# Row-wise maximum of absolute values of an 8192 x 8192 matrix: tile loads issued from two queues in turn

## The chip, the core and the metric

The kernel runs on one core of a Trainium2 chip. The metric is the device time of one execution in microseconds (us): lower is better. Three runs of the kernel before gave 634.45, 634.63 and 634.87 us, so the median is 634.63 us. Beside these timed runs there is one profiled execution, and every duration below comes from that one. Its span, from the first to the last instruction, is 632.9 us.

## What is computed

The reference takes the infinity norm of every row, which is the largest absolute value in the row:

```python
def setup_inputs():
    return {
        "x": np.random.randn(8192, 8192).astype(np.float32),
    }

def reference(x: np.ndarray) -> np.ndarray:
    return np.linalg.norm(x, ord=np.inf, axis=1)
```

The input has 8192 x 8192 x 4 B = 268.4 MB and every byte is read once. The output is 8192 numbers, 32 KB.

## The kernel before

**Tiling.** The 8192 rows are cut into 64 tiles of 128 rows. Row p of a tile lies in partition p of the on-chip memory, so a whole tile is 128 partitions of 8192 numbers (32 KB in each partition, 4 MB in all). This text counts the tiles from 0 to 63. Tiles live in `xt`, from a pool of five buffers (line 39): tile t takes the buffer that tile t - 5 had, and its first load may start only when VectorE has finished reading that older tile.

**Loop.** For each tile the loop at line 48 walks over the chunks of its columns. For each chunk it issues one load (line 55, on the queue of SP, the engine SyncE) and then one VectorE reduction (line 59), which takes the maximum of the absolute values along the row. Tiles 0 to 53 have one chunk of 8192 columns, and their reduction writes directly into column t of the result tile `res`. The last ten tiles follow the list `COOLDOWN` (line 11):

```python
COOLDOWN = (
    [[4096, 4096]] * 7
    + [[4096, 2048, 2048]]
    + [[2048, 2048, 2048, 2048]]
    + [[2048, 2048, 1536, 1280, 1280]]
)
```

Tiles 54 to 60 have two chunks, tile 61 three, tile 62 four and tile 63 five. The reduction of chunk h of such a tile writes column h of a small tile `partial`, which has five columns and only one buffer (line 46). All ten tiles share it. After its last chunk, each of these tiles has one more VectorE reduction (line 68) that takes the maximum over the used columns of `partial` and writes column t of `res`. This text writes "61 h2" for chunk 2 of tile 61, counting chunks from 0.

**Order.** No order is written out by hand. A framework turns the loop into one instruction list for each engine and adds the waits: a reduction waits for its load, a load waits for the reader of the buffer that it overwrites, and a reduction that writes a column of `partial` waits for the line 68 reduction that read that column for the tile before. Loads report to eight completion semaphores in turn, so that load n also waits for load n - 8. The list for VectorE holds 54 whole-tile reductions, then 26 chunk reductions with ten line 68 reductions between them, in the order of the source. The list for SP holds 80 loads, also in the order of the source, and at its end the store of the output.

**End.** After the last tile `res` (128 x 64) is transposed by TensorE (line 78), copied out of its accumulator by VectorE (line 80) and stored by one DMA (line 81). ScalarE (ACT) has no work in this kernel.

Of the kernel before, what the change touches and what calls it, by code (L numbers as in the profile page):

```python
# [1 line left out]

# [5 lines left out]
# [10 lines that stand above are left out]
@with_exitstack  # L19
def kernel(  # L20
    ctx: ExitStack,
    tc: tile.TileContext,
    x: bass.AP,
    out: bass.AP,
):
    nc = tc.nc
    P = 128
    n_rows, n_cols = x.shape
    assert n_rows % P == 0

    T = n_rows // P
    if n_cols == 8192 and T >= len(COOLDOWN):
        chunks = [[n_cols]] * (T - len(COOLDOWN)) + COOLDOWN
    else:
        chunks = [[n_cols]] * T

    x_t = x.rearrange("(t p) m -> t p m", p=P)

    pool = ctx.enter_context(tc.tile_pool(name="sbuf", bufs=5))
    single = ctx.enter_context(tc.tile_pool(name="single", bufs=1))  # L40
    psum_pool = ctx.enter_context(tc.tile_pool(name="psum", bufs=1, space=bass.MemoryType.PSUM))

    res = single.tile([P, T], mybir.dt.float32)
    maxch = max(len(c) for c in chunks)
    if maxch > 1:
        partial = single.tile([P, maxch], mybir.dt.float32)

    for t in range(T):
        ch = chunks[t]
        assert sum(ch) == n_cols  # L50
        xt = pool.tile([P, n_cols], x.dtype)
        off = 0
        for h, w in enumerate(ch):
            dst = res[:, t : t + 1] if len(ch) == 1 else partial[:, h : h + 1]
            nc.sync.dma_start(  # L55
                out=xt[:, off : off + w],
                in_=x_t[t, :, off : off + w],
            )
            nc.vector.tensor_reduce(  # L59
                out=dst,  # L60
                in_=xt[:, off : off + w],
                axis=mybir.AxisListType.X,
                op=mybir.AluOpType.max,
                apply_absolute_value=True,
            )
            off += w
        if len(ch) > 1:
            nc.vector.tensor_reduce(  # L68
                out=res[:, t : t + 1],
                in_=partial[:, : len(ch)],  # L70
                axis=mybir.AxisListType.X,
                op=mybir.AluOpType.max,
            )

    ident = single.tile([P, P], mybir.dt.float32)
    make_identity(nc, ident)
    res_t_psum = psum_pool.tile([T, P], mybir.dt.float32)
    nc.tensor.transpose(res_t_psum, res, ident)  # L78
    res_t = single.tile([T, P], mybir.dt.float32)
    nc.vector.tensor_copy(out=res_t, in_=res_t_psum)  # L80
    nc.sync.dma_start(out=out.rearrange("(t p) -> t p", p=P), in_=res_t)


# [1 line left out]
_INS = ['x']  # L85
_OUTS = [((8192,), 'float32')]


# [23 lines left out]
```

## Time and profile before

| Quantity | Value |
|---|---|
| Median of three runs | 634.63 us (634.45 to 634.87) |
| Span of the profiled execution | 632.9 us |
| Bytes read by the loads | 268.44 MB, mean 424 GB/s over the span |
| VectorE (DVE) busy | 558.9 us, 88% of the span |
| Whole-tile reductions | 54, mean 8686 ns |
| Chunk reductions of 4096 / 2048 / 1536 / 1280 columns | mean 4416 / 2278 / 1742 / 1476 ns |
| Reductions over `partial` (line 68) | 10, mean 156 ns |
| Whole-tile loads, from issue to landing | 54, median 39.8 us |
| Issue of one load on SP | 80, median 328 ns |

The difference between the median and the profiled span is 634.63 - 632.9 = 1.73 us, which lies around the span. A load's time from issue to landing includes the time that it stands behind earlier loads, so 39.8 us is not what the transfer of one tile takes. "Idle before" in a row of the profile is the time that the engine stood still just ahead of those instructions, with what ended it.

### The profile page before, as it was taken

How to read it: one execution, taken by the hardware profiler on the slowest of the kernel's cores; microseconds unless marked ns; L12 is line 12 of the kernel's file. 1: busy time of each engine (PE TensorE's matmuls, PEld its weight loads, DVE VectorE, ACT ScalarE, POOL GpSimd, SP SyncE). 2: the span in 40 equal slices, each digit the busy share in tenths (PEclk: the TensorE clock that was granted, in tenths of full speed). 3: DMA queues.
4: the chain of work that ended last, by engine and by line, in shares of the span. 5: the costliest groups of instructions: out<-in, count | busy, mean ns of one | idle time of the engine just before them, and what ended most of it. 6: DMA issues, size and time to landing. Idle time of an engine off the chain costs nothing.

```text
span 632.9 us, 294 instructions
## 1 busy us (share of the span) xinstructions
PE 0.4 (0%) x1; PEld 0.1 (0%) x1; DVE 558.9 (88%) x91; POOL 0.7 (0%) x6
## 2 busy tenths in 40 slices
PE   0000000000000000000000000000000000000000
PEld 0000000000000000000000000000000000000000
DVE  1988988988989889889898898898988989999997
POOL 0000000000000000000000000000000000000000
DMA  8999999999999999999999999999999999999995
GB/s 373 439 437 437 433 431 433 431 431 431 431 431 431 431 431 431 431 431 431 431 431 431 431 431 431 431 431 431 431 437 433 435 435 418 427 428 431 425 421 219
DMA packets 11602, 268.49 MB, mean 424 GB/s; under 512 B 1296, under 2 KB 1360, under 8 KB 1744
## 3 DMA queue, kind: packets, MB, share of 16 engines
q1 hardware_dynamic: 11600, 268.47, 98.9%
q14 instruction: 2, 0.02, 0.0%
HBM read 268.44 MB, written 0.03 MB: 424 GB/s over the span
## 4 chain that ended last, share of the span: by engine, by line
DMA 75%; DVE 24%; SPq 0%; issue 0%; PE 0%; DVEq 0%
DMA xt<-in_x_dram 75%; DVE res L59 15%; DVE partial L59 8%; SPq L55 0%; DVE res L68 0%; PE res_t_psum L78 0%; DVE res_t L80 0%; DVEq L59 0%
## 5 line engine op out<-in xcount | busy, mean ns | idle before, releaser
L59 DVE TENSOR_REDUCE res<-xt 128x1 f32<-128x8192 f32 x54 | 469.0, 8686 | 67.6 <-DMA xt<-in_x_dram 67.6
L59 DVE TENSOR_REDUCE partial<-xt 128x1 f32<-128x4096 f32 (+3 forms) x26 | 88.1, 3430 | 2.7 <-DMA xt<-in_x_dram 2.6
L68 DVE TENSOR_REDUCE res<-partial 128x1 f32<-128x2 f32 (+3 forms) x10 | 1.6, 156 | 0.3
L80 DVE COPY res_t<-res_t_psum 64x128 f32<-64x128 f32 x1 | 0.3, 283 | 0.6 <-PE res_t_psum L78 0.6
L78 PE MATMUL res_t_psum<-ident,res 128*64 128x128 f32 x1 | 0.4, 393 | 629.5 <-DVE res L68 629.5
masks.py:199 POOL TENSOR_SCALAR_AFFINE_SELECT ident<-ident 128x128 f32<-128x128 f32 x1 | 0.3, 292 | 0.1
L78 PEld LDWEIGHTS res_t_psum<-ident,res 128*64 128x64 f32 x1 | 0.1, 128 | 629.4 <-issue 629.4
masks.py:197 POOL MEMSET ident<- 128x128 f32 x1 | 0.2, 204 | 0.3 <-POOLq L96 0.3
L96 POOL MEMSET const-bfloat16-1.0<- 128x1 bf16 x1 | 0.1, 101 | 0.0
L96 POOL MEMSET const-uint8-127<- 128x1 uint8 x1 | 0.1, 101 | 0.0
L96 POOL MEMSET const-float32-0.0<- 128x1 f32 x1 | 0.1, 98 | 0.2 <-issue 0.2
L96 POOL MEMSET const-float32-1.0<- 128x1 f32 x1 | 0.1, 98 | 0.0
## 6 DMA issues: line engine op xcount, KB each, us to landing
xt<-in_x_dram SPq DMA_DIRECT2D x54, 4096.0 KB, 39.8
xt<-in_x_dram SPq DMA_DIRECT2D x15, 2048.0 KB, 38.7
xt<-in_x_dram SPq DMA_DIRECT2D x8, 1024.0 KB, 28.3
xt<-in_x_dram SPq DMA_DIRECT2D x2, 640.0 KB, 17.9
xt<-in_x_dram SPq DMA_DIRECT2D x1, 768.0 KB, 19.3
out_dram<-res_t SPq DMA_DIRECT2D x1, 32.0 KB, 1.8
```

What stands on the lines that cost most here:

```text
L59: nc.vector.tensor_reduce(out=dst, in_=xt[:, off : off + w], axis=mybir.AxisListType.X, op=mybir.AluOpType.max, apply_absolute_value=True,)
L68: nc.vector.tensor_reduce(out=res[:, t : t + 1], in_=partial[:, : len(ch)], axis=mybir.AxisListType.X, op=mybir.AluOpType.max,)
L78: nc.tensor.transpose(res_t_psum, res, ident)
L80: nc.vector.tensor_copy(out=res_t, in_=res_t_psum)
L96: nc = _bacc.Bacc("TRN2", target_bir_lowering=False, num_devices=1)
```

## The change

A counter `n_dma` is added that runs over all 80 loads. Loads with an even number are issued from SP as before, loads with an odd number from the queue of ScalarE (ACT). Nothing else in the source differs: chunk sizes, buffers, reductions and the final store (from SP) stay.

```diff
+    n_dma = 0
     for t in range(T):
...
             dst = res[:, t : t + 1] if len(ch) == 1 else partial[:, h : h + 1]
-            nc.sync.dma_start(
+            queue = (nc.sync, nc.scalar)[n_dma % 2]
+            n_dma += 1
+            queue.dma_start(
                 out=xt[:, off : off + w],
                 in_=x_t[t, :, off : off + w],
             )
```

So tiles 0 to 53 alternate between the queues as wholes. Of tiles 54 to 60 chunk 0 goes to SP and chunk 1 to ACT. Of tile 61 chunks 0 and 2 go to SP and chunk 1 to ACT. Of tile 62 chunks 1 and 3 go to SP, 0 and 2 to ACT. Of tile 63 chunks 1 and 3 go to SP, 0, 2 and 4 to ACT.

## The prediction

> **What bounds the kernel now.** I read the page first, then the windows of the end, then the chain of waits. On the page, part 2 and the two costliest groups carry it:
>
> ```profile
> DVE  1988988988989889889898898898988989999997
> DMA  8999999999999999999999999999999999999995
> GB/s 373 439 437 437 433 431 433 431 431 431 431 431 431 431 431 431 431 431 431 431 431 431 431 431 431 431 431 431 431 437 433 435 435 418 427 428 431 425 421 219
> ...
> L59 DVE TENSOR_REDUCE res<-xt 128x1 f32<-128x8192 f32 x54 | 469.0, 8686 | 67.6 <-DMA xt<-in_x_dram 67.6
> L59 DVE TENSOR_REDUCE partial<-xt 128x1 f32<-128x4096 f32 (+3 forms) x26 | 88.1, 3430 | 2.7 <-DMA xt<-in_x_dram 2.6
> ```
>
> The DMA engines are full from the second slice to the last but one, at a steady 431 GB/s. A tile of 4.194 MB takes 4.194 / 0.431 = 9.7 us to load and 8.69 us to reduce, so VectorE waits about 1 us per tile: 67.6 us in all, 12.9 of them before the first tile. The loads set the pace, and VectorE follows closely. The windows show when the last load ends (time, length, busy us of PE, PE's weight loads, VectorE and GpSimd, clock, DMA share, GB/s):
>
> ```profile
> 602.00:617.00 15.00, 0.00 (x0) 0.00 (x0) 14.85 (x7) 0.00 (x0) 1.00 1.01 421
> ...
> 617.00:620.00 3.00, 0.00 (x0) 0.00 (x0) 2.98 (x2) 0.00 (x0) 1.00 1.03 429
> 620.00:622.00 2.00, 0.00 (x0) 0.00 (x0) 1.95 (x2) 0.00 (x0) 1.00 0.99 408
> ...
> 624.00:625.00 1.00, 0.00 (x0) 0.00 (x0) 1.00 (x2) 0.00 (x0) 1.00 1.02 415
> 625.00:626.00 1.00, 0.00 (x0) 0.00 (x0) 1.00 (x1) 0.00 (x0) 1.00 0.27 108
> 626.00:627.00 1.00, 0.00 (x0) 0.00 (x0) 1.00 (x2) 0.00 (x0) 1.00 0.03 10
> ```
>
> Between 625 and 626 the share falls to 0.27, so I set the end of the loads at 625.4 us. The chain, in order of time, shows VectorE's end (start, length, what):
>
> ```profile
> 545.56 8.76 DVE partial L59 x2
> 554.31 0.02 issue
> 554.34 0.17 DVE res L68
> 554.50 0.02 issue
> 554.53 8.76 DVE partial L59 x2
> ...
> 602.09 8.82 DVE partial L59 x3
> ...
> 611.12 8.88 DVE partial L59 x4
> ...
> 620.21 8.94 DVE partial L59 x5
> 629.14 0.02 issue
> 629.17 0.17 DVE res L68
> 629.34 0.14 issue
> 629.47 0.41 PE res_t_psum L78
> ```
>
> VectorE runs without a gap over tiles 61, 62 and 63 and ends at 629.34, only 4 us after the last load. From there to the end of the span are 3.56 us of transpose, copy and store. One tile of the end costs VectorE, from its start to the next tile's: 554.53 - 545.56 = 8.97 us with two chunks, 611.12 - 602.09 = 9.03 (tile 61), 620.21 - 611.12 = 9.09 (tile 62), and 629.34 - 620.21 = 9.13 (tile 63). So little comes after the last load because VectorE reduces in the order in which loads land.
>
> **What the Trainium skill says.** "DMA: Bandwidth & Descriptors", section "Issuing engines are not separate DMA queues": loads from SP and ACT run on the same 16 DMA engines, and a second issuer saves only issue time. The trace before can't show two queues, but it agrees on the second half: an issue takes 328 ns on SP, and the DMA share is 1.00 in mid-kernel, so no issue time is exposed. The section "Queues, rings and completion order" says that each DMA engine takes turns between the queues it has work for, a packet at a time. Here the packets add up: 80 loads of 128 rows are 10,240, the store has 64 rows, and the packets under 512 B are 1,296 = 81 x 16; the sum is the 11,600 of the page. So a packet in the records is one partition's row of one load or one of 16 small ones per DMA. "HBM Reference", section "Specifications (TRN2)": a core that streams alone measures about 425 GB/s, bound by its 16 DMA engines; the trace has 424 in the mean and 431 in the steady part.
>
> **The change part by part.** *Issue.* Forty of 80 issues of 328 ns move from SP to ACT, which is otherwise empty. They lie beside full DMA engines: gain 0. At the start alone up to 0.4 us might be gained (second issue of the chain); I take 0.
>
> *Rate.* No row shows two queues. From above: the best slice has 439 GB/s instead of 431, which would end 265 MB of loads 265 / 0.431 - 265 / 0.439 = 11 us earlier. From below: the shorter rows of the end ran at 408 to 429, in the windows of 617 to 625 some 418, 3% less; if changing between queues cost as much on every row, 19 us would be lost. Since the DMA engines are busy throughout and rows keep their 32 KB, I take 0.
>
> *Landing in pairs.* Tiles 0 and 1 now share the engines and land together, near 21 us instead of 12 and 21. VectorE's first reduction starts some 9 us later, but it has 17.4 us of work for 19.4 us of loads per pair. After a pair lands three loads are still outstanding in five buffers; the first freed buffer comes after 8.7 us and the second after 17.4, both ahead of the next landing at 19.4. Each queue then still holds a load: no DMA idles. Gain and loss 0.
>
> *VectorE's order at the end.* This is where the change costs, and it isn't in the diff. I compared the built instruction lists of both kernels. Before, VectorE's list is the source's. In the changed one three reductions stand ahead of their place. From tile 58 on, with what is moved marked:
>
> ```
> 58 h0, 58 h1, [61 h2], max 58, [62 h3], 59 h0, 59 h1, [63 h4], max 59,
> 60 h0, 60 h1, max 60, 61 h0, 61 h1, max 61, 62 h0, 62 h1, 62 h2, max 62,
> 63 h0, 63 h1, 63 h2, 63 h3, max 63
> ```
>
> These three are the first users of columns 2, 3 and 4 of partial, so no earlier reader holds them back; the scheduler was free to place them early. Each waits for its own load, and VectorE stands still behind it: 62 h3 is the last chunk of tile 62, 63 h4 the last of the whole input. Queued behind 62 h3 are tiles 59, 60, most of 61, 62 and 63; after them TensorE and the store. The loads aren't held: in the built list those of tile 63 need only 58 h1, which stands ahead of all three. So the loads still end at 625.4, with VectorE idle beside them.
>
> When does 62 h3 land? Both queues have 40 loads of 128 rows. With turns row by row the loads land in pairs, one of each queue: 61 h2 (SP) with 62 h0 (ACT), 62 h1 with 62 h2, 62 h3 with 63 h0, 63 h1 with 63 h2, 63 h3 with 63 h4. After 62 h3 there remain 2048 + 1536 + 1280 + 1280 = 6144 columns, 6144 x 512 B = 3.15 MB, at 418 GB/s 7.5 us: it lands at 617.9. The 61 h2 ahead lands 8192 columns = 10.0 us sooner, at 607.9, is reduced in 2.2 us, and VectorE waits again. 63 h4 costs no wait: VectorE reaches it at 617.9 + 2.2 + 8.8 = 628.9, after 625.4.
>
> From 617.9 VectorE has everything from tile 59 on but 61 h2: 2 x 8.97 + 9.03 + 9.09 + 9.13 - 2.22 (a quarter of 8.88) = 42.97 us. It ends at 617.9 + 43.0 = 660.9 instead of 629.34: 31.5 us later. Span 632.9 + 31.5 = 664.4; with the 1.73 us around the span, 666.1 us. The extra semaphore waits in the lists (17 ns each in the trace before) are below 0.2 us together.
>
> The landing of 62 h3 is bounded from both sides: with loads served in the order of issue all of tile 63 (10.0 us) follows it, which gives 615.4 and 663.6 us; with equal bytes to both queues SP, with 2560 columns more than ACT from tile 61 on, ends last, and 3.1 us alone plus 1.9 us shared follow: 620.4 and 668.6 us. I take the middle, since the packet count supports turns by row.
>
> **The rivals.** *Rate better, still slower*: with 439 GB/s all of the end moves up by 11 us, to 655 us. The early slices of 437 to 439 speak for it; DMA share 1.00 at 431 speaks against. *Rate worse, or a starved queue*: up to 19 us more, 685 us. For it: 418 on short rows. Against: rows stay as long as before and each queue keeps a load. *The order does no harm*: VectorE's moved reductions would have to be absent in the run. Then only the pairs act: 61 h0 and h1 land together some 2.4 us later than 61 h0 did at 602.0 (2048 columns, 2.5 us), and VectorE's unbroken 27.3 us end at up to 631.8: 634.6 to 637.1 us. Against: the list is what the engine executes, and the trace before follows its list. *Not slower*: two queues on each DMA engine would have to raise the load rate so far that the late loads land 31.5 us earlier. The place is the whole steady stretch, the point is 268.4 MB / 593 us = 453 GB/s; below it the kernel stays slower. No slice of the profile exceeds 439.
>
> **How the numbers follow.** Forecast, 660 to 673 us: 0.80. Rate better, 650 to 660: 0.07. Rate worse, 673 to 685: 0.09. Order harmless, 634.6 to 637: 0.02. Rate above 453: 0.02. The likeliest is 666 us. The range holds the landing's bounds (663.6 to 668.6) and about 0.7% of the load time on either side for the rate, 4 to 5 us: 659 to 674. A change under 0.2% can't be told from none here. Faster has the last case, 0.02; same takes half of the harmless order, 0.01; slower 0.97.
>
> **What would show it.** VectorE should stand idle in two long stretches between about 590 and 618, released by loads, with the DMA share still near 1 to about 625; then some 43 us of reductions without a gap and no load beside them after 625. Whole-tile reductions should wait in pairs, near 2 us before every second one. Reductions should keep 8.69 us and the steady rate 431 GB/s. I am wrong if the loads end more than 5 us from 625.4, if 63 h4 rather than 62 h3 is the last long wait, or if VectorE's tail is short.

## The result, and the profile after

The changed kernel takes 667.62 us (four runs, 667.31 to 667.69) beside 634.54 us for the kernel before in the same comparison: a ratio of 1.052, 95% interval 1.0505 to 1.0535. Its profiled execution has a span of 665.9 us. The prediction was 666 us, range 659 to 674.

The page of the changed kernel, the lines that answer to those shown of the kernel before:

```profile
DVE  0688889888888988888898888889888899941797
DMA  9999999999999999999999999999999999999500
GB/s 378 441 441 419 431 441 431 419 441 437 421 433 441 431 419 441 433 423 435 441 427 423 441 433 419 439 441 425 425 441 431 419 428 430 428 426 421 230 0 2
...
L62 DVE TENSOR_REDUCE res<-xt 128x1 f32<-128x8192 f32 x54 | 466.5, 8681 | 78.4 <-DMA xt<-in_x_dram 78.4
L62 DVE TENSOR_REDUCE partial<-xt 128x1 f32<-128x4096 f32 (+3 forms) x26 | 87.9, 3429 | 27.9 <-DMA xt<-in_x_dram 27.6
```

The reductions cost what they did (8681 ns against 8686). The DMA engines are as full as before, but they are done two slices before the end, and VectorE has a hole in the slices 36 and 37, while they are still full, that reaches into slice 38. The idle time ahead of the chunk reductions has grown from 2.7 to 27.9 us. The timeline of the same execution (start, length, engine, line, what, count, and in brackets the idle time ahead of it with what ended it) shows where:

```profile
580.74 8.75 DVE L62 TENSOR_REDUCE partial<-xt 128x1 f32<-128x4096 f32 x2
609.52 2.29 DVE L62 TENSOR_REDUCE partial<-xt 128x1 f32<-128x2048 f32 x1 [20.03 <-DMA xt<-in_x_dram]
611.73 0.14 DVE L71 TENSOR_REDUCE res<-partial 128x1 f32<-128x2 f32 x1
619.46 12.34 DVE L62 TENSOR_REDUCE partial<-xt 128x1 f32<-128x2048 f32 x4 [7.59 <-DMA xt<-in_x_dram]
...
662.17 0.16 DVE L71 TENSOR_REDUCE res<-partial 128x1 f32<-128x5 f32 x1
```

At 580.74 VectorE reduces the two chunks of tile 58. Then it waits 20.03 us for one chunk of 2048 columns, 61 h2, finishes tile 58, and waits 7.59 us more for 62 h3. The group "x4" that starts at 619.46 is 62 h3, 59 h0, 59 h1 and 63 h4. From there it runs without a gap until 662.33. The loads are over long before, as the windows of the changed kernel show (columns as in the prediction):

```profile
624.00:625.00 1.00, 0.00 (x0) 0.00 (x0) 1.00 (x1) 0.00 (x0) 1.00 1.02 415
625.00:626.00 1.00, 0.00 (x0) 0.00 (x0) 1.00 (x2) 0.00 (x0) 1.00 0.24 92
...
630.00:666.00 36.00, 0.39 (x1) 0.13 (x1) 32.33 (x19) 0.00 (x0) 1.00 0.00 1
```

So the loads end when they ended before, and 662.33 - 619.46 = 42.9 us of reductions, most of which used to lie beside the loads, now lie behind the wait.

### The profile page after: what moved, and what is told of

It reads as the page before. It is cut to its first block, busy times and chain, and to the rows that moved or that the text cites. A ratio compares the mean times of both kernels' runs of the same rounds, so it can differ in the third digit from the quotient of the medians.

```text
span 665.9 us, 303 instructions
## 1 busy us (share of the span) xinstructions
PE 0.4 (0%) x1; PEld 0.1 (0%) x1; DVE 556.0 (83%) x91; POOL 0.7 (0%) x6
## 4 chain that ended last, share of the span: by engine, by line
DMA 64%; DVE 35%; issue 1%; another core or an unknown queue 0%; PE 0%; SPq 0%
DMA xt<-in_x_dram 64%; DVE res L62 26%; DVE partial L62 8%; DVE res L71 0%; PE res_t_psum L81 0%; SPq L58 0%; DVE res_t L83 0%
## 5 line engine op out<-in xcount | busy, mean ns | idle before, releaser
L62 DVE TENSOR_REDUCE res<-xt 128x1 f32<-128x8192 f32 x54 | 466.5, 8681 | 78.4 <-DMA xt<-in_x_dram 78.4
L62 DVE TENSOR_REDUCE partial<-xt 128x1 f32<-128x4096 f32 (+3 forms) x26 | 87.9, 3429 | 27.9 <-DMA xt<-in_x_dram 27.6
## 6 DMA issues: line engine op xcount, KB each, us to landing
xt<-in_x_dram ACTq DMA_DIRECT2D x1, 768.0 KB, 19.5
```

Of the source, the lines that this page charges most:

```text
L62: nc.vector.tensor_reduce(out=dst, in_=xt[:, off : off + w], axis=mybir.AxisListType.X, op=mybir.AluOpType.max, apply_absolute_value=True,)
```

## The experiments

All of them leave the chunks, the buffers and what each load brings alone. In all but experiment 2, a change in which columns of `partial` are read decides which reductions the scheduler can place early: a reduction that writes a column must stay behind an earlier reader of that column. `partial` is zeroed at the start, and a maximum of absolute values isn't changed by a zero that is read too.

**1. Two queues, VectorE in the order of the source.**

```diff
         partial = single.tile([P, maxch], mybir.dt.float32)
+        nc.gpsimd.memset(partial, 0.0)
...
-                in_=partial[:, : len(ch)],
+                in_=partial[:, :maxch],
```

> Two queues as in the change, but VectorE's list in the order of the source: every reduction over partial reads all five columns (zeroed at the start), so that no chunk reduction can be placed ahead of the tile before it. Theory (the order of VectorE's list is the whole loss): 634.6 to 637.1 us, no wait at the end over 3 us, loads landing until about 627. Rival (two queues cost by themselves, through pairs of tiles landing late or slower loads): most of the loss stays, 650 to 668 us.

Measured: 640.40 us, ratio 1.0091 (1.0076 to 1.0106). Of the 33.1 us, 27.2 are gone with the order alone, and VectorE waits for no load after 527.8 us. The last wait, and the end of VectorE's reductions:

```profile
527.80 17.28 DVE L63 TENSOR_REDUCE res<-xt 128x1 f32<-128x8192 f32 x2 [2.14 <-DMA xt<-in_x_dram]
...
634.87 0.16 DVE L72 TENSOR_REDUCE res<-partial 128x1 f32<-128x5 f32 x1
```

But 5.7 us remain (640.4 - 634.7), more than the 2.4 that the theory allowed and less than the 15 that the rival asked for, so both missed. Experiments 6 and 7 go after the 5.7 us.

**2. One queue, VectorE in the order of the changed kernel.** The loop is written out from tile 58 on, all loads stay on SP, and an ordering edge without a wait ties each reduction from tile 58 on to the one ahead of it.

```diff
...
+    for t in range(59, 64):
+        load(t)
+    chunk(61, 2)
+    last(58)
+    chunk(62, 3)
+    chunk(59, 0)
+    chunk(59, 1)
+    chunk(63, 4)
+    last(59)
...
```

> One queue (SP) for all loads, but VectorE's list in the order that the changed kernel has (61 h2, 62 h3 and 63 h4 ahead of their places). Theory: 62 h3 lands with only tile 63 behind it, 10.0 us ahead of the last landing at 627.1, so at 617.1; 43.0 us of reductions follow: span 663.7, time 665.4 us, some 2 us below the changed kernel. Rival (the second queue is needed for the loss): 634.6 us.

Measured: 665.16 us, ratio 1.048 (1.0465 to 1.0496), 0.2 us from the theory. Its timeline:

```profile
607.04 2.29 DVE L77 TENSOR_REDUCE partial<-xt 128x1 f32<-128x2048 f32 x1 [25.06 <-DMA xt<-in_x_dram]
609.25 0.15 DVE L88 TENSOR_REDUCE res<-partial 128x1 f32<-128x2 f32 x1
616.98 12.33 DVE L77 TENSOR_REDUCE partial<-xt 128x1 f32<-128x2048 f32 x4 [7.59 <-DMA xt<-in_x_dram]
```

The loss appears without a second queue. 62 h3 lands at 616.98, 2.5 us sooner than with two queues, because in one queue only tile 63 stands behind it.

**3 to 5. One moved reduction at a time, two queues.** Each run lets one of the three reductions go ahead of its place. The columns of `partial` that chunks 2, 3 and 4 use are exchanged so that the free one is the last (for 61 h2 and 62 h3), and the tiles ahead read the others:

```diff
+COL = [0, 1, 2, 4, 3]
...
-            dst = res[:, t : t + 1] if len(ch) == 1 else partial[:, h : h + 1]
+            dst = res[:, t : t + 1] if len(ch) == 1 else partial[:, COL[h] : COL[h] + 1]
...
-                in_=partial[:, : len(ch)],
+                in_=partial[:, : 4 if len(ch) < 4 else 5],
```

This is the one for 62 h3. For 61 h2 the list is `[0, 1, 4, 2, 3]` and the condition `len(ch) < 3`; for 63 h4 there is no list, and the tiles read at least four columns.

Only 61 h2:

> Two queues; of the three reductions only 61 h2 stands ahead of its place (the columns of chunks 2, 3 and 4 are exchanged and the earlier tiles read those of chunks 3 and 4 too). Theory (the end is a landing plus the work still queued behind it, and only the worst counts): landing 609.5 + 45.2 of work + 3.56 + 1.73 = 660.0 us. Rival (each wait adds its own idle time, 20.0 us here): 634.5 + 20.0 = 654.5 us.

Only 63 h4:

> Two queues; only 63 h4, the last chunk of the input, stands ahead of its place, now between the chunks and the maximum of tile 60. Theory: VectorE idles until it lands at 627.1, then has 0.2 + 9.03 + 9.09 + 9.13 = 27.45 us left: 654.6 + 3.56 + 1.73 = 659.8 us, though the changed kernel shows no wait at all for this chunk. Rival (what costs nothing in the changed kernel costs nothing alone): 634.6 to 637 us.

Only 62 h3:

> Two queues; of the three reductions only 62 h3 stands ahead of its place, between the chunks and the maximum of tile 58, as in the changed kernel. Theory (a landing plus all the work still queued behind it): 619.4 + 45.2 + 3.56 + 1.73 = 669.9 us, 2.2 us slower than the changed kernel, because 61 h2 is then no longer reduced inside the wait. Rival (the idle time that this wait had in the changed kernel is its price): 634.6 + 7.6 = 642 us.

Measured: 660.28 us with 61 h2 alone (ratio 1.0404, 1.0387 to 1.0421), 659.89 us with 63 h4 alone (1.0397, 1.0382 to 1.0413), and 670.08 us with 62 h3 alone (1.0557, 1.0542 to 1.0571). All three stand within 0.3 us of the theory. The rivals had been put on a base of 634.5 to 637 us; with the order restored the base is 640.4 (experiment 1). On that base the rival for 61 h2 gives 640.4 + 20.0 = 660.4, so this run doesn't tell the two apart. The other two do: 640.4 and 648.0 would have been the rival's times for 63 h4 and 62 h3, and 659.89 and 670.08 were measured. One timeline line of each kernel, in the same sequence:

```profile
609.44 2.29 DVE L66 TENSOR_REDUCE partial<-xt 128x1 f32<-128x2048 f32 x1 [19.80 <-DMA xt<-in_x_dram]
```

```profile
626.88 1.49 DVE L63 TENSOR_REDUCE partial<-xt 128x1 f32<-128x1280 f32 x1 [19.39 <-DMA xt<-in_x_dram]
```

```profile
619.28 2.29 DVE L66 TENSOR_REDUCE partial<-xt 128x1 f32<-128x2048 f32 x1 [29.67 <-DMA xt<-in_x_dram]
```

Compare the brackets with those of the changed kernel. Ahead of 61 h2 the idle time is the same, 19.80 against 20.03 us. Ahead of 62 h3 it is 29.67 instead of 7.59, and ahead of 63 h4 it is 19.39 where the changed kernel shows none. VectorE's work is the same in all of them, so each kernel takes 640.4 us plus the idle time of its own trace: 640.4 + 29.67 = 670.1, for example. But how long that idle time is depends on which early instruction stands first, and what it shows in company says little of what it costs alone. What holds throughout is the landing of the awaited chunk plus the work queued behind it; where several chunks are awaited, the latest of these ends counts. In the changed kernel that is the one of 62 h3, since 61 h2 and 63 h4, which alone end near 660 us, lie before it. With 62 h3 alone the kernel is even 2.5 us slower than with all three moved, since 61 h2 is then no longer reduced inside the idle time (2.2 us by the theory).

**6. The body on two queues, the end on one.** VectorE's order is that of the source, as in experiment 1.

```diff
-            queue = (nc.sync, nc.scalar)[n_dma % 2]
+            queue = (nc.sync, nc.scalar)[n_dma % 2 if t < 54 else 0]
```

> VectorE's list in the order of the source; tiles 0 to 53 alternate between the two queues, tiles 54 to 63 are all on SP. The question is what the 5.7 us of the run with two queues and the source's order are. Theory (the pairs leave VectorE one whole tile behind at 527.8, 8.6 us, of which the end can work off only the 2.9 us that VectorE idles there in the kernel before): the same 640.4 us. Rival (halves of one tile that land together on two queues at the end): back to 634.7 us.

Measured: 640.30 us, ratio 1.0087 (1.0074 to 1.0101). The halves of a tile that land together at the end aren't the cause, since here all of the end is on one queue. The timeline at the hand-over, first this kernel's, then the kernel before's:

```profile
527.78 17.28 DVE L63 TENSOR_REDUCE res<-xt 128x1 f32<-128x8192 f32 x2 [2.16 <-DMA xt<-in_x_dram]
544.98 8.73 DVE L63 TENSOR_REDUCE partial<-xt 128x1 f32<-128x4096 f32 x2
```

```profile
518.28 8.69 DVE L59 TENSOR_REDUCE res<-xt 128x1 f32<-128x8192 f32 x1 [1.02 <-DMA xt<-in_x_dram]
527.99 8.69 DVE L59 TENSOR_REDUCE res<-xt 128x1 f32<-128x8192 f32 x1 [1.03 <-DMA xt<-in_x_dram]
536.60 8.73 DVE L59 TENSOR_REDUCE partial<-xt 128x1 f32<-128x4096 f32 x2
```

Tiles 52 and 53 landed together, so VectorE starts tile 54 at 544.98 instead of 536.60, 8.4 us late. Before, it idles 2.6 us over the ten tiles that follow. It can work off no more than that, and 8.4 - 2.6 = 5.8 us are left; 5.6 were measured (640.3 - 634.7).

**7. The change of queues ten tiles sooner.** As experiment 6 with `t < 44`.

> The same with the change of queues ten tiles earlier: tiles 0 to 43 alternate, tiles 44 to 63 are all on SP. Theory: the tile that VectorE is behind is worked off at 9.71 - 8.69 = 1.0 us per whole tile over ten tiles, so 634.5 to 635 us and again a wait at 602. Rival (a fixed cost of having used a second queue at all): 640 us.

Measured: 634.70 us, ratio 0.9998 (0.999 to 1.0006): no difference. After its last pair VectorE reduces nine tiles without a wait, from 430.56 us on. From 508.29 the waits ahead of single tiles are back, among them the one at 602:

```profile
518.01 8.69 DVE L63 TENSOR_REDUCE res<-xt 128x1 f32<-128x8192 f32 x1 [1.04 <-DMA xt<-in_x_dram]
...
602.19 8.81 DVE L63 TENSOR_REDUCE partial<-xt 128x1 f32<-128x4096 f32 x3 [0.35 <-DMA xt<-in_x_dram]
```

With 44 tiles on two queues nothing is lost, and nothing gained. The remaining cost of the pairs is therefore the one tile that VectorE is behind at the hand-over. It vanishes where the tiles that follow leave enough idle time to work it off.

## Why the prediction was right

**The order of VectorE's list.** The forecast put the loss into three reductions ahead of their places. Restoring the order with two queues removes 27.2 us (experiment 1), and moving them with one queue produces 30.4 (experiment 2). Both directions are shown. Why the scheduler moves them only in the changed kernel was not pursued.

**The sum.** Forecast 617.9 + 42.97 = 660.9 for VectorE's end; the trace has 619.46 + 42.87 = 662.33. The work was right to 0.1 us, and the 3.56 us after it came out as forecast (665.9 - 662.33 = 3.57). The 1.5 us between 666.1 and 667.6 lie in one term, the landing: both moved chunks that are waited for came 1.6 us later than worked out (609.52 against 607.9, 619.46 against 617.9). The first pair, put near 21 us, was late too: its reductions start at 22.45. The sum counted back from 625.4, where the mean share of the 16 DMA engines falls off. VectorE's wait for a chunk ends later than that. The kernel with 63 h4 moved shows the size, since there VectorE waits for the last chunk of all. Its windows:

```profile
624.00:625.00 1.00, 0.00 (x0) 0.00 (x0) 0.00 (x0) 0.00 (x0) 1.00 0.99 404
625.40:625.50 0.10, 0.00 (x0) 0.00 (x0) 0.00 (x0) 0.00 (x0) 1.00 0.39 154
626.00:626.20 0.20, 0.00 (x0) 0.00 (x0) 0.00 (x0) 0.00 (x0) 1.00 0.06 26
626.20:626.40 0.20, 0.00 (x0) 0.00 (x0) 0.00 (x0) 0.00 (x0) 1.00 0.01 0
```

The bytes don't stop at one moment. The share fades, the last packet is recorded between 626.20 and 626.25, and the reduction starts at 626.88. The share of 0.06 after 626.00 is that of one engine out of 16. So of the 1.5 us from 625.4, some 0.8 are DMA engines that finish later than the others, and the reduction starts 0.6 to 0.7 us after the last packet. 62 h3 lands 626.88 - 619.46 = 7.4 us ahead of this last chunk. Turns by row had given 7.5 us.

**Turns by row.** The bounds were service in the order of issue, 10.0 us ahead of the end, and equal bytes to both queues, 5.0 us ahead. The measured 7.4 us lie between them. The packets show the turns too. Here are the DMA queues of the changed kernel in the window 597.5 to 600 (packets, MB, share), where SP sends rows of 16 KB (61 h0) against rows of 8 KB on ACT (61 h1):

```profile
q1 hardware_dynamic: 44, 0.72, 68.0%
q10 hardware_dynamic: 45, 0.37, 35.0%
```

Both queues are served side by side, the packets are equal, and the bytes are not. This agrees with the section of the Trainium skill that the prediction named, "Queues, rings and completion order" in "DMA: Bandwidth & Descriptors". How many rows make up one turn these counts don't show.

**Rate and issue at nothing.** Between 52 and 536 us the mean is 432 GB/s in both kernels, first the kernel before, then the changed one:

```profile
52.00:536.00 484.00, 0.00 (x0) 0.00 (x0) 433.34 (x50) 0.00 (x0) 1.00 1.00 432
```

```profile
52.00:536.00 484.00, 0.00 (x0) 0.00 (x0) 430.18 (x50) 0.00 (x0) 1.00 1.00 432
```

The rivals with a better or worse rate fall. That a second issuing engine brings no second set of DMA engines, as "Issuing engines are not separate DMA queues" in the same page of the Trainium skill states, agrees with these equal rates. No issue time is gained either: with 44 tiles on two queues the kernel takes 634.70 us beside 634.69 (experiment 7).

**Landing in pairs at nothing.** This was right for the changed kernel and wrong as a general statement, and that it did no harm was luck: the prediction asked whether the DMA engines idle, and not how far VectorE is behind when the pairs end. The pairs appear as forecast (2.16 us of waiting ahead of every second tile), and the DMA engines don't starve. But VectorE reaches the end of the body one tile late. In the changed kernel the 20.03 us of idle time before 61 h2 cover that; with the order restored it costs 5.7 us. The rival "the order does no harm", put at 634.6 to 637.1 us, was mis-sized for the same reason: it counted the pair of chunks in tile 61 and not the pair of tiles 52 and 53.

**63 h4 without a wait.** Right: VectorE reaches it near 630.5, 3.6 us after its landing. Yet alone it costs 19.5 us (659.89 against 640.40 with the order restored).

## What to carry to other kernels

Changing who issues a transfer can change what a scheduler does with the engines that consume it, so compare the instruction lists of the consumers, not the diff alone. An instruction that stands too early in an in-order list sets the end at the landing it waits for plus all the work queued behind it; where there are several, the latest of these ends counts, and the idle time shown ahead of one isn't what it would cost alone (7.59 us became 29.67, and none became 19.39). Where one consumer follows a stream closely, two queues that take turns make neighbours land together, and the consumer is one item behind at the end. It catches up only as far as the items that follow leave it idle time: the last ten tiles through one queue changed nothing here (640.30 us), the last twenty restored the time (634.70 us).

## What the hardware showed that was not expected

The 16 DMA engines don't finish the last load together. In the kernel with 63 h4 moved their mean share is 0.99 until 625 and 0.39 between 625.4 and 625.5, and the last packet is recorded between 626.20 and 626.25. The reduction that waits for it starts at 626.88, 0.6 to 0.7 us after that packet.

Two queues with rows of different length don't share the bandwidth equally. With rows of 16 KB against 8 KB they had 44 and 45 packets, but 0.72 and 0.37 MB.

The load rate of the changed kernel swings between 419 and 441 GB/s over slices of 16.6 us in the body, where the kernel before held 431 in most slices. This isn't the work of the second queue: experiment 2, with one queue, swings between 413 and 443, and experiment 1, with two, between 427 and 443. The means over 484 us are equal. The cause of the swing was not tested.
